# Two token blocks share one score product in a chunked recurrence: half of the blocks held backwards

## The chip, the cores and the metric

One core of a Trainium2 chip runs the whole program. The metric is the time of one execution on the device, in microseconds, as the median of several runs. Beside the runs there is one execution that the hardware profiler took; its rows are those shown below.

## The reference, cut to what matters

The model is a trunk of two layers over 1024 tokens of width 1024, all in float32. The first layer's mixer has two parallel parts, a gated linear recurrence with four heads and a sliding-window attention with eight; the second layer's mixer pools. A gated MLP with a short convolution follows each mixer and takes most of the time. The change touches the mixer of the first layer alone:

```
f = lb + (1 - lb) * sigmoid(fz);   k = (1 - lb) * sigmoid(-fz)
b = cumsum(log f) inside a chunk
att[t, s] = sum_k q[t, k] * k[s, k] * exp(b[t, k] - b[s, k])     for s <= t, else 0
o[t] = (q[t] * exp(b[t])) @ S + sum_s att[t, s] * v[s]
S    = exp(b_last) * S + sum_s (k[s] * exp(b_last - b[s])) v[s]
```

```
window attention: scores of a block of 128 queries against its own
and the previous 128 keys; allowed where 0 <= query - key < 128;
softmax with a learned sink; times the values
```

## The kernel before, in words

Tokens are worked in two halves of 512 (`hf`), a half in four blocks of 128 (`c` or `t`). Activations lie with features on the partitions and the half's 512 tokens along the free axis.

**The recurrence.** For each head and half, `head_in` (line 518) makes the gate `f`, the keys `k`, the queries `q`, the queries times the gate `q1`, and values with output gates `z`. `mixer_head` (line 783) then works through the scores in a binary tree, so that no exponentials of long sums are needed. A first product (the call at line 795) gives the diagonal. After that come seven levels, m = 1, 2, 4, ... 64. At level m each block is cut into groups of 2m tokens; queries in the second half of a group meet keys in the first half. The helper `level` (line 788) makes four 128 x 128 products, one for each block, over all keys `K` and all queries `Q` (`q1`); each product is two instructions on TensorE, since the type is float32. On VectorE line 810 multiplies the second-half queries, line 811 the first-half keys by the decay that they gain on the way to the next level, line 814 makes the next decays `tot`, and line 816 copies those scores into `att` that belong to this level, by the mask `lmask`. Three quarters of what a level's products compute is thrown away: only 64 keys and 64 queries of a block meet.

```python
ps = level(K, Q)
V.tensor_tensor(view(Q, 1), view(Q, 1), t_first.broadcast_to([P, nb, m]), ALU.mult)
V.tensor_tensor(view(K, 0), view(K, 0), t_second.broadcast_to([P, nb, m]), ALU.mult)
V.copy_predicated(view(att, 1), lmask[...], view(ps, 1))
```

There are 4 heads x 2 halves x 7 levels = 56 levels, and 8 diagonal products.

After the levels, `ktp` (line 825) turns the keys, `up` (line 834) makes the state updates, `ho` (lines 850 and 852) the outputs, line 858 squares them for the norm, and `join_head` (line 874) turns the result by a transposition and splits it for the output projection.

**The window attention.** `mixer_swa` (line 644) rotates queries and keys, transposes them (`kp`, `qp`), makes the scores `sc` (line 690), adds the mask `smask` and takes the maximum (line 699, VectorE), exponentiates (line 715, ScalarE: eight instructions for each block of queries, with a sum each), divides, transposes the probabilities (`tpz`) and multiplies by the values.

**What sets the order.** Both parts are generators. The big products (`gemm`, line 302, and the loops of `head_in`) call `tick`, which advances each active generator by one `yield`, so that a level stands between pieces of the big products. The framework's scheduler then orders the instructions of each engine at build time; the engines run their queues strictly in that order. Weights are fetched two pieces ahead (`fetch`, `weight`), and each piece is split by ScalarE and VectorE (line 298).

Of the kernel before, what the change touches and what calls it, by code (L numbers as in the profile page):

```python
# [9 lines left out]
F32 = mybir.dt.float32  # L10
# [4 lines left out]
ALU = mybir.AluOpType  # L15
# [46 lines left out]
def trunk(ctx: ExitStack, tc: tile.TileContext, a: dict, out: bass.AP):  # L62
# [26 lines left out]

    def ax(name):  # L90
        return pa.tile([P, 512], F32, tag="ax", name=name)

    def col(t, i):
        return t[:, i : i + 1]
# [315 lines left out]
    def load_h0(hf):  # L410
        for k in range(KT):
            x = t2("x0")
            nc.sync.dma_start(x, a["xT"][hf, k])
            modulate(x, k, s0, t0, h0[hf])
            yield


    def first_h0():
        for k in range(KT):
            for ch in (1, 0):  # L420
                ada_tile(0, ch, k, b4("adast"))
                ada_bias(0, ch, k, k + 1)
            V.tensor_scalar(col(s0, k), col(mods[0, 1], k), 1.0, None, ALU.add)
            x = t2("x0")
            nc.sync.dma_start(x, a["xT"][0, k])
            modulate(x, k, s0, t0, h0[0], act=k > 0)
            yield

# [135 lines left out]
    z_swa, pf = first_in()  # L564

    ident = load("ident", [P, P])
    lng = load("ln_gT", [P, 4 * KT])
    lnb = load("ln_bT", [P, 4 * KT])
    cvw = [load(f"cw{l}", [P, 3 * FT], src=a["conv_w"][l]) for l in range(DEPTH)]
# [5 lines left out]
    for i in range(2):  # L575
        st = wp.tile([P, 1024], F32, tag="ws", name="lmst", bufs=WS_BUFS)
        nc.sync.dma_start(st[:, :896], a["lmask"][:, i * 896 : (i + 1) * 896])
        V.tensor_copy(lmask[:, i * 896 : (i + 1) * 896], st[:, :896])
    smask = load("smask", [P, 256])
    normg = load("norm_g", [P, P], src=a["norm_g"].broadcast_to([P, P]))  # L580
    sink = load("sinks", [P, 8], src=a["sinks"].broadcast_to([P, 8]))
    nsink = cp.tile([P, 8], F32, tag="nsink", name="nsink")
# [13 lines left out]


    posi = load("pos", [P, 8], I32)
    posf = cp.tile([P, 8], F32, tag="posf", name="posf")
    V.tensor_copy(posf, posi)  # L600
    freq = load("freq", [P, 8], src=a["freq"].broadcast_to([P, 8]))
    ang = cp.tile([P, 8, 8], F32, tag="ang", name="ang")
    kk = cp.tile([P, 8, 8], F32, tag="kk", name="kk")
    sin = cp.tile([P, 8, 8], F32, tag="sin", name="sin")
    cos = cp.tile([P, 8, 8], F32, tag="cos", name="cos")
    V.tensor_tensor(
# [19 lines left out]
    kTs = {}  # L626
    zkv = {}
    states = {}

    def rope(z, nh, hf):  # L630
        c = cos[:, hf * NT : (hf + 1) * NT, :].unsqueeze(2).broadcast_to([P, NT, nh, 8])
# [12 lines left out]
    def mixer_swa(z, hf):  # L644
# [17 lines left out]
        def queries(t):  # L662
            qp = ax("qp")
            for j in range(4):
                PE.transpose(qp[:, j * P : (j + 1) * P], z[j // 2][:, t, (j % 2) * P : (j % 2 + 1) * P], ident)
            qT = t2("qT")
            S.copy(qT, qp)
            return qT

        def scores(t, qT):  # L670

            blk = hf * NT + t
            if blk == 0:
                srcs = [(1, 1, kT[:, 0:P])]
            elif t == 0:
                srcs = [(0, 1, kTs[hf - 1][:, HT - P : HT]), (1, 1, kT[:, 0:P])]
            else:
                srcs = [(0, 2, kT[:, (t - 1) * P : (t + 1) * P])]  # L680
            lo = P if blk == 0 else 0
            mxs, ngm, rs, es = (sm([P, 8], nm, 2) for nm in ("mxs", "ngm", "rs", "es"))
            p = [b4("pt").rearrange("p (j k) -> p j k", j=4) for _ in range(2)]
            for jj in range(0, 4, 2):
                sp_ = [ax("sc"), ax("sc")]
                for j in (jj, jj + 1):
                    for b0, nb, src in srcs:
                        for kv in range(2):
                            rows = slice(kv * 64, kv * 64 + 64)
                            PE.matmul(  # L690
                                sp_[kv][:, (j - jj) * 256 + b0 * P : (j - jj) * 256 + (b0 + nb) * P],
                                qT[rows, j * P : (j + 1) * P],
                                src[rows, :],
                                start=True,
                                stop=True,
                            )
                for kv in range(2):
                    for j in (jj, jj + 1):
                        V.tensor_tensor_reduce(
                            out=p[kv][:, j, lo:256],  # L700
                            in0=sp_[kv][:, (j - jj) * 256 + lo : (j - jj) * 256 + 256],
                            in1=smask[:, lo:256],
                            scale=0.125,
                            scalar=NEG,
                            op0=ALU.add,
                            op1=ALU.max,
                            accum_out=col(mxs, kv * 4 + j),
                        )
# [74 lines left out]
    def mixer_head(st, hd, hf):  # L783
# [1 line left out]
        tot = t2("tot")  # L785
        att = t2("att")

        def level(lhs, rhs):
            ps = ax("att")
            for c in range(NT):  # L790
                s = slice(c * P, (c + 1) * P)
                PE.matmul(ps[:, s], lhs[:, s], rhs[:, s], start=True, stop=True)  # L792
            return ps

        ps = level(K, q)
        V.tensor_tensor(
            att.rearrange("p (c t) -> p c t", c=NT),
            ps.rearrange("p (c t) -> p c t", c=NT),
# [1 line left out]
            ALU.mult,  # L800
        )
        yield
        cur, off = f, 0
        for li, m in enumerate(LEVELS):
            nb = HT // (2 * m)
            ps = level(K, Q)
            view = lambda t, i: t.rearrange("p (b two m) -> p b two m", two=2, m=m)[:, :, i, :]
            pr = cur.rearrange("p (b two) -> p b two", two=2)
            t_first, t_second = pr[:, :, 0:1], pr[:, :, 1:2]
            V.tensor_tensor(view(Q, 1), view(Q, 1), t_first.broadcast_to([P, nb, m]), ALU.mult)  # L810
            V.tensor_tensor(view(K, 0), view(K, 0), t_second.broadcast_to([P, nb, m]), ALU.mult)
            nxt = tot[:, off : off + nb]
            off += nb
            V.tensor_tensor(nxt.unsqueeze(2), t_first, t_second, ALU.mult)
            cur = nxt
            V.copy_predicated(
                view(att, 1),
                lmask[:, li * 256 : (li + 1) * 256].rearrange("p (b m) -> p b m", m=m),
                view(ps, 1),
            )  # L820
            yield

# [30 lines left out]
            if c == 1:  # L853
                yield
        ssq = sm([P, NT], "ssq", 2)
        junk = sm([P, P], "junk", 1)
        for c in range(NT):
            S.activation(junk, op[:, c * P : (c + 1) * P], AF.Square, accum_out=col(ssq, c))
        V.tensor_scalar(ssq, ssq, 1.0 / P, RMS_EPS, ALU.mult, ALU.add)
        y = rsqrt(ssq, NT, "rms")  # L860
        sg = f
# [12 lines left out]
    def join_head(hf, hd):  # L874
        o = o_hl[hf]
        ps = ax("ogT")
        for c in range(NT):
            s = slice(c * P, (c + 1) * P)
            PE.transpose(ps[:, s], og[hf, hd][:, s], ident)
        split(o[hd][:, 0, :], o[hd][:, 1, :], ps)  # L880

    def join_swa(hf):
# [436 lines left out]
def _layout(i):  # L1319
# [2 lines left out]
    f = {}  # L1322
    x = i["x"][0]
    f["xT"] = c(x.T.reshape(KT, P, NH, HT).transpose(2, 0, 1, 3))
    f["c"] = c(i["c"].reshape(1, D))
    f["ada_wT"] = c(i["ada_w"].transpose(0, 2, 1).reshape(DEPTH, 48, P, D))
    f["ada_bT"] = c(i["ada_b"].reshape(DEPTH * 48, P).T)
# [17 lines left out]
    f["lb_raw"] = c(i["hgrn_lb_raw"][0].reshape(4, P).T)  # L1345
    f["norm_g"] = c(i["hgrn_norm_g"].reshape(1, P))
    f["sinks"] = c(i["attn_sinks"].reshape(1, 8))
    f["pos"] = c(i["positions"][0].reshape(8, P).T)
    f["pool_w"] = c(i["pool_w"][0].reshape(2, 2, 2, P, 256).transpose(0, 3, 1, 2, 4).reshape(2, P, 1024))
    f["pscaleT"] = c(i["pool_scale"][0].reshape(KT, P).T)  # L1350
    f["w_up"] = c(i["ffn_w_up"].reshape(DEPTH, KT, P, 2 * FT, P).transpose(0, 3, 2, 1, 4).reshape(DEPTH, 2 * FT, P, 1024))
# [2 lines left out]
    f["w_dn"] = c(i["ffn_w_down"].reshape(DEPTH, FT, P, KT, P).transpose(0, 3, 2, 1, 4).reshape(DEPTH, KT, P, FF))  # L1354

    f["ident"] = np.eye(P, dtype=np.float32)
    s = np.arange(P)
    masks = []
    for m in LEVELS:
        b = np.arange(P // (2 * m))  # L1360
        on = (s[:, None] // (2 * m) == b[None, :]) & (s[:, None] % (2 * m) < m)
        masks.append(np.tile(np.repeat(on[:, :, None], m, axis=2).reshape(P, 64), (1, NT)))
    f["lmask"] = np.concatenate(masks, axis=1).astype(np.float32)
    q, k = np.arange(P)[:, None] + P, np.arange(2 * P)[None, :]
    rel = q - k
    f["smask"] = np.where((rel >= 0) & (rel < P), 0.0, NEG).astype(np.float32)
    f["freq"] = (np.float32(500000.0) ** (-np.arange(0, 16, 2, dtype=np.float32) / np.float32(16))).astype(np.float32).reshape(1, 8)
    t = np.arange(16)
    f["icnt"] = np.stack([w / np.minimum(t + 1, w) for w in (2, 4, 8, 16)]).astype(np.float32).reshape(1, 4, 16)
# [19 lines left out]
```

## Time and profile before

| what | value |
|---|---|
| runs (3), median, lowest and highest | 1935.89 us, 1933.04 to 1939.52 us |
| the profiled execution | 1936.9 us |
| its span, first to last instruction | 1935.1 us |
| instructions | 25764 |
| mean granted TensorE clock over the span | 0.993 of full speed |

The profiled execution's own time is 1.0 us above the median of the runs and 1.8 us above its span. Busy time of TensorE includes overlap of neighbouring matmuls, so what one costs is read from the distance between starts in the timeline, not from its duration. The mixer of the first layer runs from about 60 to 450 us of the span.

### The profile page before, as it was taken

How to read it: one execution, taken by the hardware profiler on the slowest of the kernel's cores; microseconds unless marked ns; L12 is line 12 of the kernel's file. 1: busy time of each engine (PE TensorE's matmuls, PEld its weight loads, DVE VectorE, ACT ScalarE, POOL GpSimd, SP SyncE). 2: the span in 40 equal slices, each digit the busy share in tenths (PEclk: the TensorE clock that was granted, in tenths of full speed). 3: DMA queues.
4: the chain of work that ended last, by engine and by line, in shares of the span. 5: the costliest groups of instructions: out<-in, count | busy, mean ns of one | idle time of the engine just before them, and what ended most of it. 6: DMA issues, size and time to landing. Idle time of an engine off the chain costs nothing.

```text
span 1935.1 us, 25764 instructions
## 1 busy us (share of the span) xinstructions
PE 1872.6 (97%) x9390; PEld 1552.5 (80%) x9390; DVE 1389.6 (72%) x2656; ACT 906.7 (47%) x1430; POOL 0.2 (0%) x4
## 2 busy tenths in 40 slices
PE   7999999999999999999999999999899999999996
PEld 6888987888777777788878888887788888878886
DVE  7797678778768887877755784898778787634506
ACT  4664244423666444344432544666554554523422
POOL 0000000000000000000000000000000000000000
PEclk9999999999999999999999999999999999999998
DMA  9622332224687556543698857448544444866861
GB/s 343 223 105 77 109 121 88 88 99 162 240 299 258 178 174 210 181 153 117 244 321 315 291 175 282 163 161 325 205 156 149 152 153 153 282 229 250 321 217 44
DMA packets 139807, 377.96 MB, mean 195 GB/s; under 512 B 17185, under 2 KB 20257, under 8 KB 139681
## 3 DMA queue, kind: packets, MB, share of 16 engines
q1 hardware_dynamic: 127008, 353.78, 52.5%
q10 hardware_dynamic: 12672, 22.55, 3.1%
q8 instruction: 73, 1.20, 0.3%
q14 instruction: 54, 0.43, 0.1%
HBM read 289.24 MB, written 87.03 MB: 194 GB/s over the span
## 4 chain that ended last, share of the span: by engine, by line
PE 72%; DVE 13%; DMA 10%; ACT 3%; issue 2%; SPq 0%; DVEq 0%; ACTq 0%
PE pd L1162 21%; PE py L1016 13%; PE pz L1016 9%; PE px L1016 8%; PE op L307 3%; DMA wst<-in_w_up 3%; PE zt L549 3%; PE att L792 3%; PE zt L431 2%; DMA wst<-g 2%; DVE whl L298 2%; PE pd L307 2%; DVE uc L963 2%; DVE adast L153 1%; PE aq L307 1%
## 5 line engine op out<-in xcount | busy, mean ns | idle before, releaser
L1016 PE MATMUL py<-t,whl 128*128 128x512 f32 x1584 | 380.5, 396 | 14.7 <-DVE v L1126 9.1
L1016 PEld LDWEIGHTS py<-t,whl 128*128 128x128 f32 x1584 | 298.2, 189 | 88.8 <-DVE v L1126 14.5
L298 ACT CAST whl<-wst 128x1024 fp32r<-128x1024 f32 (+2 forms) x199 | 201.2, 1020 | 280.3 <-PE pd L1162 93.6
L1162 PE MATMUL pd<-gh,whl 128*128 128x512 f32 x1024 | 321.5, 391 | 1.9 <-ACT gh L298 1.9
L298 DVE TENSOR_TENSOR whl<-wst,whl 128x1024 fp32r<-128x1024 f32 (+2 forms) x199 | 233.7, 1183 | 94.8 <-ACT whl L298 93.8
L1016 PE MATMUL px<-hf,whl 128*128 128x512 f32 x1056 | 250.5, 393 | 7.6 <-ACT s L1056 2.9
L1016 PEld LDWEIGHTS px<-hf,whl 128*128 128x128 f32 x1056 | 198.4, 189 | 52.1 <-ACT s L1056 3.7
L1162 PEld LDWEIGHTS pd<-gh,whl 128*128 128x128 f32 x1024 | 192.4, 188 | 42.7 <-ACT gh L298 2.4
L1162 PE MATMUL pd<-gl,whl 128*128 128x512 f32 x512 | 200.1, 391 | 0.2 <-DVE gl L298 0.2
L153 DVE CUSTOM_DVE_ANT_0 adast<-adast,c 128x1024 f32<-128x1024 f32 x96 | 116.7, 1221 | 39.4 <-DMA adast<-in_ada_wT 39.2
L1016 PE MATMUL pz<-t,whl 128*128 128x512 f32 x528 | 131.6, 395 | 1.9 <-ACT whl L298 1.3
L1016 PE MATMUL pz<-hf,gs 128*128 128x512 f32 x528 | 130.1, 395 | 0.0
L963 DVE SCALAR_TENSOR_TENSOR uc<-u,cw,uc 128x511 f32<-128x511 f32 (+1 forms) x160 | 119.0, 744 | 5.7 <-ACT uc L960 5.7
L1016 PEld LDWEIGHTS pz<-t,whl 128*128 128x128 f32 x528 | 98.6, 187 | 26.9 <-ACT whl L298 1.8
L1016 PEld LDWEIGHTS pz<-hf,gs 128*128 128x128 f32 x528 | 99.4, 188 | 23.4
L1162 PEld LDWEIGHTS pd<-gl,whl 128*128 128x128 f32 x512 | 96.5, 189 | 21.0 <-DVE gl L298 0.9
L1162 PE MATMUL pd<-gt,whl 128*128 128x512 f32 x432 | 103.6, 394 | 0.7 <-DVE gt L298 0.7
L549 PE MATMUL zt<-whl,h 128*128 128x256 f32 x768 | 100.0, 286 | 0.0
L1162 PEld LDWEIGHTS pd<-gt,whl 128*128 128x128 f32 x432 | 80.7, 187 | 21.1 <-DVE gt L298 1.2
L1172 DVE SCALAR_TENSOR_TENSOR r<-pd,mod,r 128x512 f32<-128x512 f32 x32 | 23.1, 749 | 101.9 <-PE pd L1162 101.9
L549 PEld LDWEIGHTS zt<-whl,h 128*128 128x128 f32 x768 | 94.3, 191 | 0.7 <-issue 0.3
L970 ACT ACTIVATE uc<-uc 128x512 f32<-128x512 f32 x88 | 55.6, 632 | 82.7 <-DVE uc L965 57.6
(243 smaller groups left out, 2677.0 us busy)
## 6 DMA issues: line engine op xcount, KB each, us to landing
wst<-in_w_up SPq DMA_DIRECT2D x126, 512.0 KB, 4.1
adast<-in_ada_wT SPq DMA_DIRECT2D x96, 512.0 KB, 4.5
wst<-in_w_dn SPq DMA_DIRECT2D x64, 512.0 KB, 5.7
wst<-g SPq DMA_DIRECT2D x44, 512.0 KB, 5.2
g<-uc SPq DMA_DIRECT2D x80, 256.0 KB, 2.1
r<-r SPq DMA_DIRECT2D x64, 256.0 KB, 4.0
wl<-whl SPq DMA_DIRECT2D x32, 512.0 KB, 3.1
whl<-wl SPq DMA_DIRECT2D x32, 512.0 KB, 4.9
```

The source lines that it names most:

```text
L153: V.tensor_tensor_reduce(out=w, in0=w, in1=cb, scale=1.0, scalar=0.0, op0=ALU.mult, op1=ALU.add, accum_out=col(mods[l, ch], k),)
L298: return S.copy(hi, src), V.tensor_tensor(lo, src, hi.bitcast(F32), ALU.subtract)
L307: PE.matmul(ps, w[wi][:, k * P : (k + 1) * P], act(k, hi), start=i == 0, stop=i == n - 1)
L431: PE.matmul(ps[t // 2][:, (t % 2) * 256 : (t % 2 + 1) * 256], h[k][:, hi, t * P : (t + 1) * P], w[wi][:, (k % 4) * 256 : (k % 4 + 1) * 256 ...
L549: PE.matmul(ps[:, u * 256 : (u + 1) * 256], h[k_][:, hi, (t + u) * P : (t + u + 1) * P], w[k_ // 4][wi][:, (k_ % 4) * 256 : (k_ % 4 + 1) * ...
L792: PE.matmul(ps[:, s], lhs[:, s], rhs[:, s], start=True, stop=True)
L963: V.scalar_tensor_tensor(uc[:, sh:], u[:, : HT - sh], cw, uc[:, sh:], ALU.mult, ALU.add)
L970: S.activation(uc, uc, AF.Silu)
L1016: PE.matmul(ps, w[wi][:, k * P : (k + 1) * P], blk[k][hi], start=start and k == pi == 0, stop=stop and k == HK - 1 and pi == 2, skip_group ...
L1162: PE.matmul(ps[jj], w[jj][wi][:, (k - c0) * P : (k - c0 + 1) * P], act(k, hi), start=k == pi == 0, stop=k == sum(last_k) - 1 and pi == 2,)
L1172: V.scalar_tensor_tensor(n[j], ps[jj], col(mods[l, 5], j), n[j], ALU.mult, ALU.add)
```

## The change

Blocks 2 and 3 of each half (`c % 4 >= 2`) are held backwards, last token first, all through the mixer: a new input `xM` is `xT` with these blocks reversed, positions are reversed alike, and a second transposition matrix `flip` (the identity with its columns reversed) takes the place of `ident` where queries enter the scores and where head outputs leave (`turned`). The masks of the window attention get a reversed twin, `smask` grows from 256 to 512 columns.

In a reversed block the first-half keys stand where a forward block has second-half ones. So at each level ScalarE copies the 64 first-half keys of block c and the 64 of block c + 2, interleaved by m, into one 128-column tile `km` (in the tile `q`, which is free by then; two buffers, by the level's parity). One product of this tile with 64 queries of block c and 64 of block c + 2 serves both: two products for a level instead of four. The queries are read in place, m at a time, and a product's 128 columns are written to PSUM in two runs of 64. VectorE's instructions keep their number of elements; the scores now lie side by side in PSUM. The keys' multiplication is written ahead of the queries'.

```diff
-            ps = level(K, Q)
+            firsts = lambda t: spread_ap(t, 0, [[2 * P + m, 2], [2 * m, nh], [1, m]])
+            seconds = lambda t: spread_ap(t, m, [[2 * P - m, 2], [2 * m, nh], [1, m]])
+            ps = ax("att")
+            km = q[:, (li % 2) * 256 : (li % 2 + 1) * 256]
+            S.copy(
+                km.rearrange("p (b w m) -> p b w m", w=2, m=m), spread_ap(K, 0, [[2 * m, nh], [2 * P + m, 2], [1, m]])
+            )
+            for c in range(2):
+                PE.matmul(
+                    ps[:, 0:256].rearrange("p (w c x) -> p w c x", w=2, c=2)[:, :, c, :],
+                    km[:, c * P : (c + 1) * P],
+                    spread_ap(Q, c * P + m, [[2 * P - m, 2], [2 * m, n1], [1, m]]),
+                    start=c == 0,
+                    stop=c == 1,
+                )
-            V.tensor_tensor(view(Q, 1), view(Q, 1), t_first.broadcast_to([P, nb, m]), ALU.mult)
-            V.tensor_tensor(view(K, 0), view(K, 0), t_second.broadcast_to([P, nb, m]), ALU.mult)
+            V.tensor_tensor(firsts(K), firsts(K), t_second, ALU.mult)
+            V.tensor_tensor(seconds(Q), seconds(Q), t_first, ALU.mult)
...
-                view(ps, 1),
+                ps[:, 0:256].rearrange("p (w b m) -> p w b m", w=2, m=m),
...
+    def spread_ap(t, offset, dims):
+        return bass.AP(tensor=t.tensor, offset=t.offset + offset, ap=[t.ap[0]] + dims)
...
+    def turned(t):
+        return flip if t >= 2 else ident
...
-            PE.transpose(ps[:, s], og[hf, hd][:, s], ident)
+            PE.transpose(ps[:, s], og[hf, hd][:, s], turned(c))
...
+    flip = load("flip", [P, P])
...
-    smask = load("smask", [P, 256])
+    smask = load("smask", [P, 512])
...
-        junk = sm([P, P], "junk", 1)
-            S.activation(junk, op[:, c * P : (c + 1) * P], AF.Square, accum_out=col(ssq, c))
+            S.activation(f[:, 0:P], op[:, c * P : (c + 1) * P], AF.Square, accum_out=col(ssq, c))
```

The scheduler places the new order. On TensorE, head 0 of the first half, before: twelve rows that begin with the product of level m = 8 and end with that of m = 32 (`att` is a level's product, `zt` and `af` are big products, `tpz` and `qp` belong to the window attention).

```order
L792 MATMUL att<-q_741,k 128x128 x4
L733 MATMUL tpz<-ident,pt 128x128 x4
L549 MATMUL zt<-whl,h_0_1_101 128x256 x2
L549 MATMUL zt<-whl,h_0_2_102 128x256 x3
L549 MATMUL zt<-whl,h_0_3_103 128x256 x3
L549 MATMUL zt<-whl,h_0_4_104 128x256
L792 MATMUL att<-q_741,k 128x128 x4
L733 MATMUL tpz<-ident,pt 128x128 x4
L549 MATMUL zt<-whl,h_0_4_104 128x256 x2
L549 MATMUL zt<-whl,h_0_5_105 128x256 x3
L549 MATMUL zt<-whl,h_0_6_106 128x256 x2
L792 MATMUL att<-q_741,k 128x128 x4
```

The same engine and head in the changed kernel: the last twelve rows up to the product of level m = 16 (the product of m = 8 stands two rows ahead of the first, with `tpz` between).

```order
L311 MATMUL af<-h_0_0_100,whl 128x512 x2
L311 MATMUL af<-h_0_1_101,whl 128x512 x3
L311 MATMUL af<-h_0_2_102,whl 128x512 x3
L311 MATMUL af<-h_0_3_103,whl 128x512 x3
L311 MATMUL af<-h_0_4_104,whl 128x512 x3
L311 MATMUL af<-h_0_5_105,whl 128x512 x3
L311 MATMUL af<-h_0_6_106,whl 128x512 x3
L311 MATMUL af<-h_0_7_107,whl 128x512 x3
L311 MATMUL aq<-h_0_0_100,whl 128x512 x3
L311 MATMUL aq<-h_0_1_101,whl 128x512 x3
L311 MATMUL aq<-h_0_2_102,whl 128x512 x2
L835 MATMUL att<-q_740,q 128x2x64 x2
```

Two products stand where there were four, and between two levels there are now 31 big products of 512 columns instead of nine or seven of 256.

On ScalarE, the same place of the changed kernel, from the copy of the keys for m = 8 to those for m = 16, 32 and 64 (`L831` is the new copy; `pt,rs<-pt,ngm` are the exponentials of one block of the window attention, `whl` is a weight's split).

```order
L831 COPY q<-k 128x256
L563 COPY zh_0_1149<-zt 128x512
L302 CAST whl<-wst 128x1024
L733 ACT_TABLE_LOAD
L733 ACTIVATE es<-es 128x8
L736 ACTIVATE pt,rs<-pt,ngm 128x256 x8
L391 ACTIVATE h_1_5_723<-x_1125,mod_87,s_99 128x512
L831 COPY q<-k 128x256
L302 CAST whl<-wst 128x1024
L831 COPY q<-k 128x256 x2
```

The copy for m = 16 has been put behind a block's eight exponentials, a table load, a weight's split and two more instructions; before, the levels used no instruction of ScalarE.

## Rows read from the trace of the kernel before

**Rows 1.** Page, part 1: busy time, share of the span, instructions of each engine

```profile
PE 1872.6 (97%) x9390; PEld 1552.5 (80%) x9390; DVE 1389.6 (72%) x2656; ACT 906.7 (47%) x1430; POOL 0.2 (0%) x4
```

**Rows 2.** Page, part 4: the chain that ended last, shares of the span by line

```profile
PE pd L1162 21%; PE py L1016 13%; PE pz L1016 9%; PE px L1016 8%; PE op L307 3%; DMA wst<-in_w_up 3%; PE zt L549 3%; PE att L792 3%; PE zt L431 2%; DMA wst<-g 2%; DVE whl L298 2%; PE pd L307 2%; DVE uc L963 2%; DVE adast L153 1%; PE aq L307 1%
```

**Rows 3.** Busy time by stretch, four slices of 10 us and the whole mixer

```profile
core 0: us, PE busy (x) PEld busy (x) DVE busy (x) ACT busy (x) POOL busy (x), PEclk, DMA share, GB/s
100.00:110.00 10.00, 9.08 (x70) 8.10 (x70) 10.00 (x36) 5.36 (x15) 0.00 (x0) 1.00 0.29 107
110.00:120.00 10.00, 10.00 (x68) 7.82 (x66) 9.98 (x27) 7.69 (x17) 0.00 (x0) 1.00 0.10 28
120.00:130.00 10.00, 10.00 (x67) 8.38 (x65) 10.00 (x35) 7.12 (x17) 0.00 (x0) 1.00 0.45 158
130.00:140.00 10.00, 9.88 (x72) 9.10 (x72) 9.95 (x32) 8.46 (x22) 0.00 (x0) 1.00 0.19 61
80.00:450.00 370.00, 364.53 (x2542) 318.17 (x2541) 286.20 (x828) 164.88 (x377) 0.00 (x0) 1.00 0.32 108
```

**Rows 4.** Timeline of TensorE: start us, us, engine line op out<-in, count

```profile
143.44 1.16 PE L792 MATMUL att<-q,k 128*128 128x128 f32 x8
144.35 3.11 PE L549 MATMUL zt<-whl,h 128*128 128x256 f32 x24
...
377.97 1.06 PE L792 MATMUL att<-q,k 128*128 128x128 f32 x8
378.78 2.32 PE L307 MATMUL aq<-h,whl 128*128 128x512 f32 x9
380.94 0.38 PE L850 MATMUL ho<-zh,att 128*128 128x128 f32 x2
```

**Rows 5.** Timeline of TensorE, first and last level product between 100 and 140 us

```profile
103.95 1.16 PE L792 MATMUL att<-q,k 128*128 128x128 f32 x8
...
137.72 1.06 PE L792 MATMUL att<-q,k 128*128 128x128 f32 x8
```

**Rows 6.** Groups by line, 60 to 500 us: count, busy us, mean ns, idle before

```profile
L738 ACT COPY pT<-tpz 128x512 f32<-128x512 f32 x14 | 8.2, 587 | 8.8 <-PE tpz L733 8.8
L715 ACT ACT_TABLE_LOAD x5 | 6.4, 1283 | 0.1
L755 ACT COPY ob<-op 128x256 f32<-128x256 f32 x16 | 5.2, 379 | 15.0 <-PE op L750 14.9
L827 ACT COPY q<-ktp 128x512 f32<-128x512 f32 x8 | 4.7, 591 | 14.2 <-PE ktp L825 14.2
L667 ACT COPY qT<-qp 128x512 f32<-128x512 f32 x8 | 4.7, 586 | 5.9 <-PE qp L665 5.9
```

**Rows 7.** Timeline of VectorE, queries at m = 1 and 64, masked copies at m = 1 and 4

```profile
89.22 0.42 DVE L810 TENSOR_TENSOR q<-q,f 128x256 f32<-128x256 f32 x1
...
116.82 0.41 DVE L810 TENSOR_TENSOR q<-q,tot 128x256 f32<-128x256 f32 x1
...
129.34 0.72 DVE L816 COPY_PREDICATED att<-lmask,att 128x256 f32<-128x256 uint8 x1
...
137.12 0.43 DVE L816 COPY_PREDICATED att<-lmask,att 128x256 f32<-128x256 uint8 x1
```

**Rows 8.** Waits of TensorE for ScalarE, 80 to 450 us: total us, times, longest

```profile
PE tpz L733 <- ACT pT L738: 1.2, 1, 1.2
...
PE sc L690 <- ACT qT L667: 0.5, 2, 0.3
```

**Rows 9.** Timeline of ScalarE, first and last of eight exponentials, what follows

```profile
107.54 0.51 ACT L715 ACTIVATE pt<-pt,ngm 128x256 f32<-128x256 f32 x1 [4.47 <-DVE ngm L710]
...
111.86 0.80 ACT L387 ACTIVATE h<-x,mod,s 128x512 fp32r<-128x512 f32 x1
...
113.29 0.59 ACT L559 COPY zh<-zt 128x512 f32<-128x512 f32 x1 [0.63 <-PE zt L549]
...
114.49 1.03 ACT L298 CAST whl<-wst 128x1024 fp32r<-128x1024 f32 x1
```

**Rows 10.** Timeline of SyncE's queue, one constant's issue

```profile
47.95 0.42 SPq L129 DMA_DIRECT2D smask<-in_smask  x1
```

More of the change, by code (lines that the diff above doesn't have):

```diff
@@ L412, in load_h0 @@
             x = t2("x0")
-            nc.sync.dma_start(x, a["xT"][hf, k])
+            nc.sync.dma_start(x, a["xM"][hf, k])
             modulate(x, k, s0, t0, h0[hf])
@@ L424, in first_h0 @@
             x = t2("x0")
-            nc.sync.dma_start(x, a["xT"][0, k])
+            nc.sync.dma_start(x, a["xM"][0, k])
             modulate(x, k, s0, t0, h0[0], act=k > 0)
@@ L598, in trunk @@
     posi = load("pos", [P, 8], I32)
-    posf = cp.tile([P, 8], F32, tag="posf", name="posf")
+    rt = t2("rot")
+    posf, freq = rt[:, 0:8], rt[:, 8:16]
+    ang, kk = (rt[:, o : o + 64].rearrange("p (b f) -> p b f", b=8) for o in (16, 80))
     V.tensor_copy(posf, posi)
-    freq = load("freq", [P, 8], src=a["freq"].broadcast_to([P, 8]))
-    ang = cp.tile([P, 8, 8], F32, tag="ang", name="ang")
-    kk = cp.tile([P, 8, 8], F32, tag="kk", name="kk")
+    nc.sync.dma_start(freq, a["freq"].broadcast_to([P, 8]))
     sin = cp.tile([P, 8, 8], F32, tag="sin", name="sin")
@@ L664, in queries @@
             for j in range(4):
-                PE.transpose(qp[:, j * P : (j + 1) * P], z[j // 2][:, t, (j % 2) * P : (j % 2 + 1) * P], ident)
+                PE.transpose(
+                    qp[:, j * P : (j + 1) * P], z[j // 2][:, t, (j % 2) * P : (j % 2 + 1) * P], turned(t)
+                )
             qT = t2("qT")
@@ L681, in scores @@
             lo = P if blk == 0 else 0
+            back = [(t - 1) % NT >= 2, t >= 2]
+            m4 = smask.rearrange("p (i b k) -> p i b k", i=2, b=2)
+            if blk == 0:
+                allowed = m4[:, 1, 0, :]
+            elif back[0] == back[1]:
+                allowed = m4[:, :, int(back[0]), :]
+            else:
+                o0, o1 = int(back[0]) * P, (2 + int(back[1])) * P
+                allowed = spread_ap(smask, o0, [[o1 - o0, 2], [1, P]])
+            blocks = (lambda v: v) if blk == 0 else (lambda v: v.rearrange("p (i k) -> p i k", i=2))
             mxs, ngm, rs, es = (sm([P, 8], nm, 2) for nm in ("mxs", "ngm", "rs", "es"))
@@ L699, in scores @@
                         V.tensor_tensor_reduce(
-                            out=p[kv][:, j, lo:256],
-                            in0=sp_[kv][:, (j - jj) * 256 + lo : (j - jj) * 256 + 256],
-                            in1=smask[:, lo:256],
+                            out=blocks(p[kv][:, j, lo:256]),
+                            in0=blocks(sp_[kv][:, (j - jj) * 256 + lo : (j - jj) * 256 + 256]),
+                            in1=allowed,
                             scale=0.125,
@@ L786, in mixer_head @@
         att = t2("att")
[L788 to L795, printed above, removed]
+        ps = ax("att")
+        for c in range(NT):
+            r = slice(c * P, (c + 1) * P)
+            PE.matmul(ps[:, r], K[:, r], q[:, r], start=True, stop=True)
         V.tensor_tensor(
@@ L805, in mixer_head @@
             nb = HT // (2 * m)
-            ps = level(K, Q)
-            view = lambda t, i: t.rearrange("p (b two m) -> p b two m", two=2, m=m)[:, :, i, :]
+            nh, n1 = nb // 2, P // (2 * m)
+            firsts = lambda t: spread_ap(t, 0, [[2 * P + m, 2], [2 * m, nh], [1, m]])
+            seconds = lambda t: spread_ap(t, m, [[2 * P - m, 2], [2 * m, nh], [1, m]])
+            ps = ax("att")
+            km = q[:, (li % 2) * 256 : (li % 2 + 1) * 256]
[9 more added lines that the diff above has]
+                    stop=c == 1,
+                )
+            t_first = spread_ap(cur, 0, [[nb + 1, 2], [2, nh], [0, m]])
+            t_second = spread_ap(cur, 1, [[nb - 1, 2], [2, nh], [0, m]])
+            V.tensor_tensor(firsts(K), firsts(K), t_second, ALU.mult)
+            V.tensor_tensor(seconds(Q), seconds(Q), t_first, ALU.mult)
             pr = cur.rearrange("p (b two) -> p b two", two=2)
-            t_first, t_second = pr[:, :, 0:1], pr[:, :, 1:2]
-            V.tensor_tensor(view(Q, 1), view(Q, 1), t_first.broadcast_to([P, nb, m]), ALU.mult)
-            V.tensor_tensor(view(K, 0), view(K, 0), t_second.broadcast_to([P, nb, m]), ALU.mult)
             nxt = tot[:, off : off + nb]
             off += nb
-            V.tensor_tensor(nxt.unsqueeze(2), t_first, t_second, ALU.mult)
+            V.tensor_tensor(nxt.unsqueeze(2), pr[:, :, 0:1], pr[:, :, 1:2], ALU.mult)
             cur = nxt
             V.copy_predicated(
-                view(att, 1),
-                lmask[:, li * 256 : (li + 1) * 256].rearrange("p (b m) -> p b m", m=m),
-                view(ps, 1),
+                seconds(att),
+                lmask[:, li * 256 : (li + 1) * 256].rearrange("p (w b m) -> p w b m", w=2, m=m),
+                ps[:, 0:256].rearrange("p (w b m) -> p w b m", w=2, m=m),
             )
@@ L1324, in _layout @@
     f["xT"] = c(x.T.reshape(KT, P, NH, HT).transpose(2, 0, 1, 3))
+    order = np.arange(T).reshape(T // P, P)
+    for b in range(T // P):
+        if b % NT >= 2:
+            order[b] = order[b][::-1]
+    f["xM"] = c(x[order.reshape(-1)].T.reshape(KT, P, NH, HT).transpose(2, 0, 1, 3))
     f["c"] = c(i["c"].reshape(1, D))
@@ L1347, in _layout @@
     f["sinks"] = c(i["attn_sinks"].reshape(1, 8))
-    f["pos"] = c(i["positions"][0].reshape(8, P).T)
+    f["pos"] = c(i["positions"][0][order.reshape(-1)].reshape(8, P).T)
     f["pool_w"] = c(i["pool_w"][0].reshape(2, 2, 2, P, 256).transpose(0, 3, 1, 2, 4).reshape(2, P, 1024))
@@ L1356, in _layout @@
     f["ident"] = np.eye(P, dtype=np.float32)
+    f["flip"] = c(f["ident"][:, ::-1])
     s = np.arange(P)
@@ L1360, in _layout @@
         b = np.arange(P // (2 * m))
-        on = (s[:, None] // (2 * m) == b[None, :]) & (s[:, None] % (2 * m) < m)
-        masks.append(np.tile(np.repeat(on[:, :, None], m, axis=2).reshape(P, 64), (1, NT)))
+        for second in (False, True):
+            on = (s[:, None] // (2 * m) == b[None, :]) & ((s[:, None] % (2 * m) >= m) == second)
+            masks.append(np.tile(np.repeat(on[:, :, None], m, axis=2).reshape(P, 64), (1, 2)))
     f["lmask"] = np.concatenate(masks, axis=1).astype(np.float32)
@@ L1365, in _layout @@
     rel = q - k
-    f["smask"] = np.where((rel >= 0) & (rel < P), 0.0, NEG).astype(np.float32)
+    sm = np.where((rel >= 0) & (rel < P), 0.0, NEG).astype(np.float32)
+    f["smask"] = np.concatenate([sm[:, :P], sm[:, :P][:, ::-1], sm[:, P:], sm[:, P:][:, ::-1]], axis=1)
     f["freq"] = (np.float32(500000.0) ** (-np.arange(0, 16, 2, dtype=np.float32) / np.float32(16))).astype(np.float32).reshape(1, 8)
```

## The prediction, as it stands on record

> **What bounds the kernel now.** First the busy shares: TensorE is busy for 97% of the span [rows 1], so a change gains by taking work from TensorE and loses by making it wait. Then the chain that ended last: the level products of line 792 are 3% of the span on it [rows 2], that is about 58 us. Then the stretches: over the whole mixer, 80 to 450 us, TensorE is busy for 364.5 of 370 us, VectorE for 286 and ScalarE for 165 [rows 3]. So TensorE bounds the mixer as well, with 5.5 us of idle time in it; ScalarE has half of its time free. VectorE is different: from 100 to 140 us it is busy for 39.93 of 40 us [rows 3], with TensorE nearly as full. There the two engines are equally late, and less work on one is not all gained. The granted clock reads 1.00 in each of these stretches [rows 3], the 2.4 GHz level, so no clock is to be won or lost.
>
> Durations below come from the profiled execution, whose own time is 1936.9 us; the median of the runs, 1935.89, is 1.0 lower.
>
> **What a level costs on TensorE, and what is removed.** Starts tell it: a level's eight instructions begin at 143.44 and the next product at 144.35, 0.91 us; at 377.97 and 378.78 it is 0.81 us [rows 4]. Half of them go: 0.405 to 0.455 us for a level. For 56 levels that is 22.7 to 25.5 us; I take 0.43, so **24.1 us less on TensorE**. This holds if an instruction with queries read in place and two runs written costs what one costs now.
>
> **Does it?** No row shows a matmul that reads or writes in pieces, so I bound it by what does. For reading: VectorE's queries at m = 1, where every second number is taken, last 0.42 us, at m = 64 0.41 us, for 256 numbers each [rows 7]; skipping costs nothing at that rate. TensorE asks for 128 columns in 0.10 to 0.11 us for each instruction, 1.2 to 1.25 numbers a nanosecond on a partition, twice VectorE's rate, so the row bounds it only loosely. But the big products of 512 columns run at 0.24 us apiece, 2.16 us for nine [rows 4], over two numbers a nanosecond; the level's products read at about half of the rate that the port gives, which leaves room for a skip. For PSUM: the masked copy that reads every second score lasts 0.72 us at m = 1, and 0.43 at m = 4, where four lie together [rows 7]. So broken access is paid for when runs are short, but from four on no more; the change writes runs of 64. I take no surcharge; the other end is that an instruction takes twice as long, 24 us in all, which eats the whole gain.
>
> The Trainium skill speaks against the change here: its page Advanced Engine Details and Errata, section Memory Cachelines, says that any PSUM pattern with gaps slows matmuls significantly, and also that pairs of neighbours suffice for full rate. No row here has such a matmul; by the first sentence the gain would be gone, by the second, with which the masked copies at m = 4 agree, nothing is lost.
>
> **What is added on ScalarE.** 56 copies of 256 numbers. The nearest row is the copy of 128 x 256 at 379 ns, from PSUM [rows 6]; 0.38 to 0.42 us each, some 22 us over the mixer, where ScalarE has 205 of 370 us free [rows 3]: its time is hidden. Its place is not. The copy has to be done before TensorE's product, and behind that product all of the big products queue. It needs the keys of the level before, and VectorE's multiplication of the keys now waits for the copy, no longer for the product; that one comes earlier, so VectorE is not held longer than now, and behind it queue the queries and the masked copy. Where TensorE today depends on ScalarE in the mixer, 8 + 14 + 8 copies [rows 6], its waits for ScalarE come to 1.7 us in all [rows 8]: 0.057 us for one. At that rate 56 new ones cost **3.2 us**. The low end is nothing; the high end is the rival on exponentials.
>
> **VectorE.** Number and size of its instructions stay. At m = 1 the masked copy may drop from 0.72 to 0.43 us, as the scores now lie together; or not, if the gaps in `att` are what costs. Between 100 and 140 us stand nine levels, the first at 103.95 and the last at 137.72 [rows 5]; TensorE's 9 x 0.43 = 3.9 us there can't all be taken while VectorE has 0.07 us to spare [rows 3]. After 140 us VectorE catches up. I take half as lost, **2 us** (0 to 3.9).
>
> **Small things.** One more constant (`flip`) and a longer one (`smask`): an issue takes 0.42 us [rows 10] ahead of the next weights in SyncE's queue, **0.5 us** (0 to 0.5). Transpositions with `flip` are as many as before. The longer distance between a head's levels (31 big products ahead of m = 16, at 0.24 us some 7.4 us) delays the head's output; the last head of the mixer still ends ahead of the second output projection in TensorE's order, under the big products of the first, so nothing waits; without that cover it would be the 7.4 us. After the mixer nothing changes; no count of transfers there depends on when the mixer ends.
>
> **The sum.** -24.1 + 3.2 + 2 + 0.5 = -18.4 us: 1936.9 - 18.4 = 1918.5 for such an execution, 1917.5 against the median. I give **1918 us**. Bounds of this case: all gained with 0.455 a level, 1910; 0.405 a level with 3.9 and 0.5 lost and twice the waits (6.4), 1925.
>
> **The rivals.**
> - *Exponentials in front of the copy (1925 to 1934).* In ScalarE's new order the keys' copy for m = 16 of the first head stands behind eight exponentials, and similar pairs recur for most of the eight blocks. The burst runs from 107.54 to 111.86, 4.3 us [rows 9]; with a table load of 1.28 us [rows 6], a value copy of 0.59, a weight's split of 1.03 and a modulation of 0.80 [rows 9] it takes 8.0 us, the copy 0.4 more. TensorE has 7.4 us of big products in between. For it: ScalarE starts a burst late, after a wait of 4.47 us for VectorE [rows 9]. Against it: the transpositions of the probabilities already hang on such bursts, and TensorE's wait for ScalarE there is 1.2 us, once [rows 8]. At 1 us a block the result is 1926, at 1.5 us 1930. Chance 0.15, four fifths of it still faster by the bound below.
> - *The chain of a level grows (slower).* Each level becomes keys on VectorE, copy on ScalarE, product on TensorE. If the copy stands bare before its product each time, that is 0.40 us, and with ScalarE busy for 165 of 370 us [rows 3] with instructions of about 0.59 us [rows 6] it finds on average 0.45 x 0.29 = 0.13 us still to run in front of it: 0.53 us a level, 29.7 us in all, and 1936.9 - 24.1 + 29.7 + 0.5 = 1943. It decides at 0.43 us of wait a level. For it: late in the mixer, levels stand with only some nine big products between them [rows 4]. Against it: the keys' copy needs only the keys, which are ready while the product before runs. Chance 0.06.
> - *Broken access costs double (1936.9 + 3.2 + 0.5, about 1941).* The 224 instructions left take as long as 448 did; what is for and against it stands above. The first sentence cited from the Trainium skill's page above would give this time. Chance 0.06, half within the bound and half above it.
> - *The change doesn't shorten TensorE's work after all,* because VectorE holds the pace through the mixer and not only from 100 to 140 us: then 1935. Against it: 84 us of VectorE's time are free in 370 [rows 3]. Chance 0.03.
>
> **How the numbers follow.** The forecast has 0.70. A measurement of this kernel tells from no change about 0.3%, 5.8 us. Faster by more: 0.70 and 0.12 of the first rival, **0.82**. Within it: 0.03 of the first rival, 0.03 of broken access, 0.03 of the last, **0.09**. Slower: 0.06 and 0.03, **0.09**. The range from 1910 to 1930 holds the forecast's bounds and most of the first rival, and leaves out what is above, about 0.18 with the tails.
>
> **What would show it.** Right: the level products' instructions fall from 448 to 224 at a distance of 0.10 to 0.11 us; the whole saving lies before 450 us of the old span; TensorE's waits for the new copies sum to a few microseconds; the new copies last about 0.4 us. Wrong: distances of about 0.2 us within a level at small m (broken access); waits of over a microsecond for ScalarE behind exponentials (first rival); short waits for it at nearly all levels (second); VectorE at ten tenths beyond 140 us (last).

## The result, and the profile after

The changed kernel takes 1915.13 us in the median of four runs (1910.85 to 1917.58), beside 1936.72 us for the kernel before: a ratio of 0.9887, 95% interval 0.9861 to 0.9913. That is 21.6 us less, where 18 us were forecast (1918, range 1910 to 1930). Timed twice more beside the kernel before, it gave 1911.91 (ratio 0.988, 0.9859 to 0.9902) and 1916.07 us (0.9895, 0.9876 to 0.9913). Runs of one kernel lie some 7 us apart, so a difference of 2 us between two kernels is not read from their medians.

The page of the changed kernel, parts 1 and 4, answers to [rows 1, 2]:

```profile
PE 1851.0 (97%) x9166; PEld 1529.8 (80%) x9166; DVE 1388.0 (72%) x2656; ACT 931.0 (49%) x1489; POOL 0.2 (0%) x4
...
PE pd L1196 20%; PE py L1050 12%; PE px L1050 9%; PE pz L1050 8%; PE op L311 4%; DMA wst<-in_w_up 4%; PE zt L553 3%; DMA wst<-g 3%; PE zt L435 2%; DVE whl L302 2%; PE pd L311 2%; DVE uc L997 2%; PE aq L311 1%; PE att L835 1%; DVE adast L157 1%
```

TensorE has 224 matmuls fewer (9390 before) and is still busy for 97%. The level products have gone from 3% to 1% of the chain (the 3% of line 792 hold the eight diagonal products as well, an eighth of its calls). VectorE has the same number of instructions, ScalarE 59 more: the 56 copies and three table loads that the new order causes.

Where the time went is read from two lines of TensorE, the head's value products `zt` and the output projection `op`, by their first and last starts. Before, and in the changed kernel (name, count, ns min/median/max, first and last start in us):

```profile
L549 PE MATMUL zt<-whl,h x768: 278/283/386, 61.9 to 399.1; 128*128 128x256 f32 x192
...
L307 PE MATMUL op<-o,whl x384: 387/389/486, 399.2 to 503.7; 128*128 128x512 f32 x192
```

```profile
L553 PE MATMUL zt<-whl,h x768: 274/283/387, 63.8 to 380.5; 128*128 128x256 f32 x192
...
L311 PE MATMUL op<-o,whl x384: 387/389/487, 380.6 to 482.5; 128*128 128x512 f32 x192
```

From the first `zt` to the last `op` the kernel before takes 503.7 - 61.9 = 441.8 us, the changed one 482.5 - 63.8 = 418.7: 23.1 us less. I call this stretch the mixer from here on. Ahead of it the changed kernel is 1.9 us later (1.1 of that in its first matmul), behind it the two differ by 1.0 us. All of the gain is made in the mixer, and since runs scatter ahead of it and behind it, the mixer's length is the sharper measure for the experiments:

| kernel | median us | ratio to before, interval | mixer in its profile, us |
|---|---|---|---|
| before | 1935.7 to 1938.3 | 1 | 441.8 |
| changed, three profiles | 1915.13, 1911.91, 1916.07 | 0.9887, 0.9880, 0.9895 | 418.7, 418.1, 420.6 |
| e2, products made twice | 1935.91 | 1.0000 (0.9988 to 1.0012) | 441.0 |
| e3, plain reading and writing | 1914.35 | 0.9882 (0.9861 to 0.9903) | 418.0 |
| e7, copies twice on ScalarE | 1913.04 | 0.9883 (0.9863 to 0.9903) | 417.3 |
| e5, copies on GpSimd | 1917.20 | 0.9912 (0.9892 to 0.9931) | 418.9 |
| e4, copies on VectorE, two jobs | 1908.14, 1908.91 | 0.9866 (0.9845 to 0.9888), 0.9862 (0.9843 to 0.9880) | 415.1, 415.0 |
| e8, copies twice on VectorE | 1915.41 | 0.9881 (0.9861 to 0.9900) | 419.2 |
| e6, scores written side by side | 1909.81, one run | not taken | 417.7 |

In the timeline of TensorE two levels: first m = 1 of the last head, where nothing is waited for, then m = 16 of the first head, the place whose order was shown ahead of the prediction:

```profile
389.06 0.62 PE L835 MATMUL att<-q,q 128*128 128x128 f32 x4
389.43 2.32 PE L311 MATMUL op<-o,whl 128*128 128x512 f32 x9
...
109.89 5.47 PE L311 MATMUL af<-h,whl 128*128 128x512 f32 x23
115.20 1.98 PE L311 MATMUL aq<-h,whl 128*128 128x512 f32 x8
117.07 0.71 PE L835 MATMUL att<-q,q 128*128 128x128 f32 x4
117.62 0.60 PE L754 MATMUL tpz<-ident,pt 128*128 128x128 f32 x4
```

In the first, the four instructions take 0.37 us to the next start, where eight took 0.81 [rows 4]: 0.44 us less. This is the level that reads its queries one at a time. Over all 56 levels of the trace, the distance from a level's first start to the next product's start runs from 0.36 to 0.65 us and adds up to 24.3 us; before, it ran from 0.81 to 1.09 and added up to 48.1. So 23.8 us went, 0.42 a level. ScalarE's timeline in front of m = 16, and the weight load for its product:

```profile
111.97 0.49 ACT L736 ACTIVATE pt<-pt,ngm 128x256 f32<-128x256 f32 x1
...
115.92 0.80 ACT L391 ACTIVATE h<-x,mod,s 128x512 fp32r<-128x512 f32 x1
116.63 0.39 ACT L831 COPY q<-k 128x256 f32<-128x256 f32 x1
```

```profile
117.07 0.52 PEld L835 LDWEIGHTS att<-q,q 128*128 128x128 f32 x4 [0.32 <-ACT q L831]
```

The copy ends at 117.02 and the product starts at 117.07, just behind its 31 big products. The copy comes a little late here: the weight load waits 0.32 us for it, while the last big products still run, and the level takes 0.55 us and not 0.37. The longest wait for a copy stands elsewhere, at m = 1 of the fifth head. There ScalarE works through a block's exponentials, a table load, two activations for a head's gate and keys and a copy of transposed probabilities before it comes to the keys:

```profile
280.58 0.50 ACT L736 ACTIVATE pt<-pt,ngm 128x256 f32<-128x256 f32 x1
...
281.19 1.28 ACT L531 ACT_TABLE_LOAD   x1
...
283.92 0.54 ACT L831 COPY q<-k 128x256 f32<-128x256 f32 x1
```

```profile
284.51 0.53 PEld L835 LDWEIGHTS att<-q,q 128*128 128x128 f32 x4 [1.22 <-ACT q L831]
```

```profile
284.51 0.72 PE L835 MATMUL att<-q,q 128*128 128x128 f32 x4 [0.80 <-ACT q L831]
```

The stretches and the groups of the changed kernel:

```profile
core 0: us, PE busy (x) PEld busy (x) DVE busy (x) ACT busy (x) POOL busy (x), PEclk, DMA share, GB/s
100.00:110.00 10.00, 9.59 (x71) 8.20 (x68) 9.73 (x35) 5.42 (x10) 0.00 (x0) 1.00 0.29 103
110.00:120.00 10.00, 10.00 (x50) 8.21 (x49) 8.71 (x25) 8.26 (x23) 0.00 (x0) 1.00 0.54 186
120.00:130.00 10.00, 10.00 (x58) 6.90 (x57) 10.00 (x31) 4.66 (x9) 0.00 (x0) 1.00 0.38 131
130.00:140.00 10.00, 10.00 (x89) 10.00 (x88) 8.69 (x30) 9.94 (x29) 0.00 (x0) 1.00 0.14 53
80.00:430.00 350.00, 345.04 (x2329) 297.53 (x2329) 286.84 (x831) 188.26 (x434) 0.00 (x0) 1.00 0.34 116
```

```profile
L835 PE MATMUL att<-q,q 128*128 128x128 f32 x224 | 36.5, 284 | 1.7 <-DVE att L851 0.8 <-ACT q L831 0.8
...
L851 DVE COPY_PREDICATED att<-lmask,att 128x256 f32<-128x256 uint8 x56 | 29.0, 519 | 0.0
L831 ACT COPY q<-k 128x256 f32<-128x256 f32 x56 | 24.0, 428 | 65.1 <-DVE k L844 26.4 <-PE att L835 11.4 <-DVE rmst L324 9.8
```

TensorE idles for 5.0 us of 350; before it was 5.5 of 370 [rows 3]. VectorE is at 37.1 of 40 us between 100 and 140 us, no longer at 39.9. Each copy lasts 0.43 us. The waits of TensorE's matmuls for ScalarE (total us, times, longest), and those of its weight loads for the copies:

```profile
PE sc L711 <- ACT qT L678: 1.0, 2, 0.7
...
PE att L835 <- ACT q L831: 0.8, 1, 0.8
```

```profile
PEld att L835 <- ACT q L831: 3.9, 7, 1.2
```

For the copies, matmuls wait 0.8 us in all, at the place just shown, and the weight loads ahead of them 3.9 us in seven places. A weight load overlaps the matmuls before it, so its wait is not lost in full: TensorE's idle time of any cause is those 5.0 us.

### The profile page after: what moved, and what is told of

It reads as the page before. It is cut to its first block, busy times and chain, and to the rows that moved or that the text cites. A ratio compares the mean times of both kernels' runs of the same rounds, so it can differ in the third digit from the quotient of the medians.

```text
span 1914.9 us, 25420 instructions
## 1 busy us (share of the span) xinstructions
PE 1851.0 (97%) x9166; PEld 1529.8 (80%) x9166; DVE 1388.0 (72%) x2656; ACT 931.0 (49%) x1489; POOL 0.2 (0%) x4
## 4 chain that ended last, share of the span: by engine, by line
PE 70%; DVE 12%; DMA 11%; ACT 4%; issue 2%; SPq 0%; DVEq 0%; ACTq 0%
PE pd L1196 20%; PE py L1050 12%; PE px L1050 9%; PE pz L1050 8%; PE op L311 4%; DMA wst<-in_w_up 4%; PE zt L553 3%; DMA wst<-g 3%; PE zt L435 2%; DVE whl L302 2%; PE pd L311 2%; DVE uc L997 2%; PE aq L311 1%; PE att L835 1%; DVE adast L157 1%
## 5 line engine op out<-in xcount | busy, mean ns | idle before, releaser
L1206 DVE SCALAR_TENSOR_TENSOR r<-pd,mod,r 128x512 f32<-128x512 f32 x32 | 23.1, 750 | 99.7 <-PE pd L1196 99.7
```

Source lines behind the costliest of these rows:

```text
L1206: V.scalar_tensor_tensor(n[j], ps[jj], col(mods[l, 5], j), n[j], ALU.mult, ALU.add)
```

## The experiments

The theory was the forecast's: TensorE's instructions set the mixer's length, the 224 that went are the gain, the copy is hidden, and broken access costs nothing. The rivals were that part of the gain has another source, that the copy stands in the chain, and that the access is paid for.

**e1, the changed kernel again, in two jobs.** No edit.

> The changed kernel once more, unedited, timed in turn with the kernel before. Theory (TensorE's instructions set the mixer's time, and the 224 that went are the gain): 20 to 25 us less, ratio 0.987 to 0.990. Rival (the gain is partly the luck of one order or one chip): under 15 us, ratio above 0.992.

> The changed kernel, unedited, as the measure for the three others on this chip: 20 to 25 us less than the kernel before.

Measured: 23.8 and 20.4 us less than the kernel before, ratios 0.9880 and 0.9895, mixers of 418.1 and 420.6 us. The first interval lies under 0.992, and the second ends under it too: the gain is there each time. Both timings have one and the same order of instructions, so they say nothing on the luck of an order; e4, e5, e7 and e8 below come in orders of their own, with mixers of 415.0 to 419.2 us.

**e2, each product made twice.**

```diff
-            for c in range(2):
+            for c in (0, 1, 0, 1):
```

> The changed kernel with each of a level's two products made twice, so that TensorE has its 448 level instructions again and all else of the change stays. Theory: the whole gain goes, 224 x 0.09 to 0.11 us = 20 to 25 us more than the changed kernel, equal to the kernel before within 5 us. Rival (part of the gain comes from the new order of keys and queries, a shorter chain on VectorE): at least 8 us faster than the kernel before.

Measured: 1935.91 us, ratio 1.0000 with an interval of 0.9988 to 1.0012, mixer 441.0 us. Its level instructions:

```profile
L835 PE MATMUL att<-q,q x448: 270/275/382, 88.5 to 426.8; 128*128 128x128 f32 x150
```

With 448 of them the time is that of the kernel before, to 0.1%, although the copies, the new order of keys and queries and the reversed blocks are all still there. So the 224 instructions are the gain, and everything else of the change together costs or gives nothing beyond the interval's 2.3 us on either side. The rival of another source falls.

**e3, plain reading and writing.**

```diff
-                    ps[:, 0:256].rearrange("p (w c x) -> p w c x", w=2, c=2)[:, :, c, :],
+                    ps[:, c * P : (c + 1) * P],
                     km[:, c * P : (c + 1) * P],
-                    spread_ap(Q, c * P + m, [[2 * P - m, 2], [2 * m, n1], [1, m]]),
+                    Q[:, c * P : (c + 1) * P],
```

> The changed kernel with the queries read as 128 neighbours and each product written as one run of 128; it leaves out the right placing of the scores, so the output is not the reference's. Theory (reading in pieces and writing two runs of 64 cost nothing): within 3 us of the changed kernel, and a level's four instructions still 0.36 to 0.38 us where nothing is waited for. Rival (broken access is paid for): over 4 us faster, and under 0.34 us a level.

Measured: 1914.35 us, between the changed kernel's own medians, mixer 418.0. TensorE's instructions stand in the changed kernel's order, one for one. A bare level of e3 in the timeline of TensorE:

```profile
387.23 0.61 PE L835 MATMUL att<-q,q 128*128 128x128 f32 x4
387.59 2.33 PE L311 MATMUL op<-o,whl 128*128 128x512 f32 x9
```

0.36 us, against 0.37 in the changed kernel at the same level, m = 1 of the last head; over all 56 levels it is 24.2 us against 24.3. Queries read m at a time and two runs of 64 written to PSUM cost nothing that shows. The rival of broken access falls.

**e7, the copy made twice on ScalarE.** The `S.copy` of the keys is written twice in a row.

> The changed kernel with each key copy made twice over on ScalarE, 56 x 0.43 = 24 us more work there, in front of the products. Theory (the copy is hidden, the products are ordered some microseconds apart): within 3 us of the changed kernel, TensorE's waits for the copies under 2 us in all. Rival (the copy stands in the chain of a level): 56 x 0.43 = 24 us slower; half of it, if every second level waits.

Measured: 1913.04 us, mixer 417.3. Both copies ran, 24.0 and 24.1 us of them:

```profile
L834 ACT COPY q<-k 128x256 f32<-128x256 f32 x56 | 24.1, 430 | 1.3
L831 ACT COPY q<-k 128x256 f32<-128x256 f32 x56 | 24.0, 429 | 49.0 <-DVE k L847 23.6 <-PE att L838 10.4 <-PE att L812 7.5
```

```profile
PE att L838 <- ACT q L834: 1.3, 3, 0.8
```

TensorE's matmuls wait 1.3 us for them instead of 0.8. Twice the copy costs nothing that shows, so it does not stand in the chain of a level: the order at build time puts other products between the levels. The rival of a longer chain falls. The rival on exponentials is borne out in one place: the wait at m = 1 of the fifth head is there again, as in every profile that has the copies on ScalarE and each product once, 0.70 to 0.85 us. A wait of this kind was there before: TensorE waited 1.2 us once for ScalarE's copy of probabilities [rows 8], and in e4 below the same level waits 0.6 to 0.7 us for that copy. At no other place do the changed kernel's matmuls wait for the copy of the keys.

**e4, the copies on VectorE, in two jobs.**

```diff
-            S.copy(
+            V.tensor_copy(
```

> The changed kernel with the 56 key copies on VectorE in place of ScalarE: VectorE gets some 56 x 0.42 = 23.5 us more work in the mixer, ScalarE 24 us less. Theory of the prediction's VectorE step (between 100 and 140 us VectorE is at its limit, so work there counts): 3 to 10 us slower than the changed kernel. Rival (VectorE has slack that the order uses, its full slices are no limit): within 3 us of the changed kernel.

> The key copies on VectorE again, beside the changed kernel on the same chip. If the earlier lead of 3.8 us is real: 2 to 6 us faster than the changed kernel once more. If it was a spread between runs: within 1.5 us of it, on either side.

Measured: 1908.14 and 1908.91 us, mixers of 415.1 and 415.0. Neither answer of the first expectation came true: with more work on VectorE the kernel was 3.8 us faster than the changed kernel of that job. The second job repeated it with 7.2 us, more than the 2 to 6 expected, and there each of the four runs (1907.53 to 1912.26) lies below each of the changed kernel's (1913.20 to 1917.84). The intervals of the ratios overlap, but both mixers are 3 us or more shorter than all three of the changed kernel. The copies and the stretches of the first job's profile:

```profile
L831 DVE COPY q<-k 128x256 f32<-128x256 f32 x56 | 16.6, 296 | 2.8 <-PE att L812 2.7
```

```profile
100.00:110.00 10.00, 10.00 (x69) 9.10 (x70) 10.00 (x36) 4.66 (x12) 0.00 (x0) 1.00 0.27 95
110.00:120.00 10.00, 10.00 (x55) 7.75 (x55) 9.51 (x30) 7.24 (x18) 0.00 (x0) 1.00 0.26 90
120.00:130.00 10.00, 10.00 (x71) 8.64 (x70) 10.00 (x37) 8.73 (x23) 0.00 (x0) 1.00 0.32 107
130.00:140.00 10.00, 9.80 (x78) 8.43 (x76) 9.84 (x33) 6.34 (x17) 0.00 (x0) 1.00 0.16 54
80.00:430.00 350.00, 345.90 (x2344) 299.57 (x2343) 299.19 (x894) 165.69 (x376) 0.00 (x0) 1.00 0.34 116
```

A copy lasts 0.30 us there, not 0.43. VectorE is full between 100 and 140 us again, 39.35 of 40, and TensorE nevertheless is busy for 39.80. So a full VectorE did not hold TensorE up. What makes e4 shorter than the changed kernel is not shown. The 3.9 us of weight loads waiting for ScalarE's copies have next to no counterpart in it, but neither do they in e8, whose mixer is as long as the changed kernel's; and the order of instructions moves in e4 as well. So the cause of these 3 to 5 us stays open.

**e8, the copies twice on VectorE.** As e4, with the copy written twice in a row.

> The key copies on VectorE and each made twice, 112 x 0.30 = 34 us of copies there in the mixer against none in the changed kernel. If VectorE still has room in its order: within 3 us of the kernel with single copies on VectorE, that is 1906 to 1912. If VectorE's limit, as the prediction saw it between 100 and 140 us, is reached now: 3 to 17 us slower than that kernel.

Measured: 1915.41 us, beside 1938.26 for the kernel before in the same job. The medians lie 6.5 to 7.3 us above e4's, but they come from different jobs; by the ratios, 0.9881 against 0.9866 and 0.9862, it is some 3 to 4 us. The mixer is 419.2, 4.1 to 4.2 us more than e4's. The second copies, and TensorE's wait for them:

```profile
L834 DVE COPY q<-k 128x256 f32<-128x256 f32 x56 | 16.4, 294 | 0.5
```

```profile
PE att L838 <- DVE q L834: 1.0, 1, 1.0
```

So 16.4 us of copies more than in e4 seem to cost about a quarter of their time, and VectorE's room seems to end here. It isn't shown beyond doubt: the intervals of the ratios overlap (0.9861 to 0.9900 against 0.9845 to 0.9888), the order of instructions moves too, and the one wait of 1.0 us explains only a part. From 80 to 430 us VectorE is busy for 309 us, in e4 299, in the changed kernel 287.

**e5, the copies on GpSimd.**

```diff
-            S.copy(
+            nc.gpsimd.tensor_copy(
```

> The changed kernel with the 56 key copies on GpSimd, which is idle in it. No row of this case shows what such a copy lasts there. If the copy's time is hidden between levels as on ScalarE (levels late in the mixer stand 2.5 to 3.5 us apart): within 3 us of the changed kernel, as long as a copy lasts under 1.5 us. Rival (a slow copy stands bare before its product): 56 x what exceeds the gap, over 10 us slower.

Measured: 1917.20 us, mixer 418.9. The median is 5.3 us above the changed kernel's of the same job, so neither the 3 us expected nor the rival's 10 came true; the intervals of the two ratios overlap by 0.001. The profiled run was the fastest of the six (1911.92), and its mixer is as long as the changed kernel's. Whether GpSimd costs a few microseconds is left open. The group of its copies:

```profile
L831 POOL COPY q<-k 128x256 f32<-128x256 f32 x56 | 39.0, 696 | 363.0 <-PE att L812 190.3 <-DVE k L844 52.2 <-PE att L835 51.0
```

Spans on GpSimd are rough; by them a copy lasts 0.70 us, 1.6 times ScalarE's, and the mixer is no longer for it.

**e6, scores written side by side.**

```diff
-                seconds(att),
+                att[:, 0:256].rearrange("p (w b m) -> p w b m", w=2, m=m),
```

> The changed kernel with the masked copy of the scores writing 256 neighbouring places of the tile in place of every second group of m; it leaves out the right placing of the scores, so the output is not the reference's. If the gaps where it writes are what made it 0.72 us at m = 1 and 2: 0.42 to 0.45 us at all levels, 29.0 us in all becoming 24. If the mask's bytes or the scores' place in PSUM made it: still 0.72 at m = 1 and 2. The whole time within 4 us of the changed kernel in both cases.

Measured, the masked copy of the changed kernel and of e6 (ns min/median/max):

```profile
L851 DVE COPY_PREDICATED att<-lmask,att x56: 419/441/745, 94.3 to 410.6; 128x256 f32<-128x256 uint8 x56
```

```profile
L851 DVE COPY_PREDICATED att<-lmask,att x56: 431/441/450, 91.7 to 407.6; 128x256 f32<-128x256 uint8 x56
```

In e6 all 56 last 0.43 to 0.45 us: the gaps where it writes made the slow ones. Gaps where it reads were gone from the changed kernel already, and had changed nothing: 29.0 us there, and 29.0 in the kernel before, where it reads every second group of scores as well:

```profile
L816 DVE COPY_PREDICATED att<-lmask,att 128x256 f32<-128x256 uint8 x56 | 29.0, 517 | 0.0
```

The group's busy time in e6 falls to 24.7 us, and the mixer, at 417.7 us, is 0.4 us under the shortest of the changed kernel: 4.3 us less on VectorE buy nothing that shows. The one run of 1909.81 us lies among the changed kernel's runs (1908.61 to 1917.84); it can't settle whether the whole stays within the expected 4 us.

## Why the prediction was right

**The mechanism, step by step.** TensorE bounds the mixer, and the change is worth the instructions that it takes away: e2 gives them back and gets the old time. The step that sized them was nearly exact: 24.1 us forecast at 0.43 a level, 23.8 measured over the 56 levels, 0.42 each. That an instruction keeps its price under broken access was taken from bounds far away, and e3 shows it to hold. So the Trainium skill's sentence that any PSUM pattern with gaps slows matmuls (page Advanced Engine Details and Errata, section Memory Cachelines) does not hold for runs of 64: 0.37 us a level with the gap, 0.36 without.

**The row used for PSUM was misread.** The prediction put the 0.72 us of the masked copy at m = 1 [rows 7] down to its reading of every second score in PSUM, and said that it might fall when the scores lie together. They lie together in the changed kernel, and the copy still lasts up to 0.745 us and 29.0 us in all; e6 shows that its writing is what costs. That the drop might not come, because of the gaps in `att`, was named as the other way. For writing to PSUM in pieces this row was the only one that the prediction had, and it measured something else; that the conclusion stood was luck in this part.

**The term that was mis-sized is VectorE's.** It was "half as lost, 2 us" of 3.9, from four full slices. A full slice is no wait, though, and the trace before the change holds next to none: all that TensorE's matmuls wait for VectorE from 100 to 140 us is

```profile
PE sc L690 <- DVE mxs L699: 0.9, 1, 0.9
```

The changed kernel's order has eased these slices (37.1 of 40), e4 fills them again with TensorE losing nothing, and e6 takes work off VectorE without a gain. So nothing of the 2 us shows. A cost appears, if e8 is read rightly, only between 16.6 and 33 us of added work. Full slices of an engine next to a full TensorE meant that its work fitted, not that it held the pace.

**ScalarE's term was too large as well.** 3.2 us were forecast from what matmuls wait; counted alike, the copies brought 0.8 us, in one place, and e7 shows that their length plays no part. The weight loads' 3.9 us are another count, which the prediction did not use, and run in part under matmuls. With the copies on VectorE the mixer is 3 to 5 us shorter; it is not shown that these waits are the reason.

**The small term** of 0.5 us for the longer constants isn't seen: the first `zt` starts at 61.9 us before, and in kernels with the same constants anywhere from 61.7 (e5) to 63.8 us.

So the forecast was 3 us too small (18.4 against 21.6) because it took off 5.7 us of losses, most of which did not come: the levels give 23.8 us and the mixer is 23.1 us shorter, which leaves 0.7 (0.1 and 2.6 in the two other profiles). Differences of this size lie within what one job's median is uncertain. Of the rivals, the first (exponentials) was closest: its wait is there once, at m = 1 of the fifth head, 0.8 us, and not for most of the eight blocks.

## What to carry to other kernels

In a stretch where one engine is busy for nearly all of the time and the queues are ordered at build time, count the instructions that a change removes from that engine, at the distance between their starts; e2's way of giving them back is a cheap test of whether that is all. Price a full second engine by the waits for it, not by its busy share. A copy that makes operands fit a shared product cost next to nothing here, as the order keeps other work between it and the product, so try it on each engine that has room: here VectorE, which looked full, was the best place, and the kernel with the copies there, 1908 to 1909 us, has the lowest medians of all that compute the whole result.

## What was not expected of the hardware

A masked copy on VectorE pays for gaps where it writes. The first head's at m = 1, 2 and 4 in the changed kernel:

```profile
94.30 0.74 DVE L851 COPY_PREDICATED att<-lmask,att 128x256 f32<-128x256 uint8 x1
...
105.23 0.72 DVE L851 COPY_PREDICATED att<-lmask,att 128x256 f32<-128x256 uint8 x1
...
107.97 0.43 DVE L851 COPY_PREDICATED att<-lmask,att 128x256 f32<-128x256 uint8 x1
```

So 256 numbers last 0.43 us when runs of four are written, and 0.72 to 0.75 us at runs of one and two, while a plain multiplication with the same gaps lasts 0.42 us at m = 1 and 0.41 at m = 64 [rows 7]. The gapped read of float32 queries by TensorE, which was the larger worry, costs nothing that shows, even one query at a time: 0.37 against 0.36 us for four instructions.
